# A hybrid trunk layer on one core: the last attention projection goes straight into the merged tiles, stores are queued when due, norm chains enter the order step by step

## The chip, the cores and the metric

One core of one Trainium2 chip. The time is that of one execution of the program in device microseconds (us); of several runs the median is given.

## What is computed

One layer over 2048 rows of width 1024: an input projection to 8208 columns, three branches (forgetting attention with 8 heads of 64, a gated delta rule with 4 heads of 128, attention over 256 memory rows), each gated and projected to width 1024, then merged, projected and normalised.

```
h = rms_norm(x, norm_g);  z = h @ w_in
(aq, ak, av, af, az, bq, bk, bv, ba, bb, bz, mq, mz, gates) = split(z)
o_a = forgetting_attention(aq, ak, av, af + b_fg)      # softmax(q k / 8 + F_q - F_k, causal) v
y_a = o_a * silu(az)
gq, gk, gv = split(silu(causal_dwconv([bq, bk, bv], conv_w)));  gq, gk l2-normalised
y_b = rms_norm(gated_delta_rule(gq, gk, gv, g_log, beta), gdn_norm_g) * silu(bz)
y_m = softmax(mq @ mk / sqrt(128)) @ mv * silu(mz)
proj = einsum('bsnc,ncd->bsnd', stack([y_a, y_b, y_m]), w_branch)
merged = sum(sigmoid(gates + b_merge) * proj, axis=branches)
out = rms_norm(x + merged @ w_out, final_norm_g)
```

## The kernel before

**Numbers.** All is float32. A product is made of three matmuls on rounded parts: high by high, high by low, low by high (`mm3k`, L393). So every operand is split: ScalarE copies the high part, VectorE or GpSimd subtracts it from the source.

**Tiles.** The rows are worked in 4 groups of 512 (g = 0 to 3). Projections are computed transposed, 128 output columns by 512 rows in one PSUM bank, with two banks ("d") in turn for all dense work. What a branch needs later goes by way of DRAM: `dkh`/`dkl` and `dv` for attention, `dgq` for the delta rule, `dgt` for the merge gates, `dya`, `dyb`, `dym` for branch outputs, `dpt` for partly merged sums.

**The order of the work** is set while the program is built. `Plan` (L24) keeps a clock for each engine: TensorE's advances by the work put in, `op`, `act`, `dve`, `pool` (L50 to L62) cost the other engines, and `dma` (L64) costs a transfer by its size at `RATE` = 250 KB per us (L35). Parts are generators; each `yield` names a time before which the part does not go on, and the clock's work. `run` (L79) takes the first part that is due and falls back on the dense stream (`dense`, L324). Each engine, and the queue of SyncE (SP) which issues every DMA, then executes its instructions in that order. `Stores` (L131) holds stores back until their planned time, used before for the projection's outputs alone (`outs`).

**The stages.** `dense` runs the input projection as jobs of 128 columns (weights `wr_in`, `wh_in`, `wl_in`). Beside it run, one after the other (`part_side`, L1282): norm, logits, memory attention, `part_gdn_a` (L720: 16 chunks of 128 rows, transposes `pk`, `pq`, `pv` and products `pa`), `part_gdn_inv` (L818: two inversions of small triangles on VectorE, 31 steps of two instructions each, L831 and L833), `part_gdn_b` (L840: the recurrence over 16 chunks; its `tail`, L970, norms a chunk's output `pO` to `ob` and transposes it to `pR`), and `part_fox` (L1001). This last is the attention: 32 units n = (head h, group G), scores `pst`, output `po` and `pq`, and `sums` (L1131), which adds up a unit's softmax denominators in `pL`, sends them through DRAM (`dL`, `lr`, `rl`, `dR`, `zl`) to turn a row into a column and back, multiplies `oS` by the result and stores it in `dya`.

The dense stream reaches the merge gates (`ev_gate`, L442), whose second half fills the attention's waits, and after them `branch` (L1422) with 8 blocks of 128 columns a group: branch 1 (delta rule) and branch 2 (memory), for each group, add gate times projection to `dpt`. For branch 0 (attention) there are two ways. Groups 0 and 1 go through `branch` too as soon as their attention units are stored: `ev_dram` (L1470) writes the full sum to `dpt[2]`. Groups 2 and 3 wait for the end of the attention and go through `branch_half` (L1538): halves u of 256 rows, two 256-column matmul blocks in one bank `pba`, whose sum is split straight into the merged tiles `mh`, `ml`. `out_half` (L1576) multiplies a half by `w_out` (`pout`), adds x, norms and stores. For groups 0 and 1 `reload_half` (L1569) brings `dpt[2]` back into merged tiles. The order of halves is 4, 5, 6, 7, 0, 1, 2, 3. `load_wo` (L1518) loads `w_out` after the attention ends.

**Loads and stores of a branch block.** `load_gate` (L1447) asks for a gate `gt` and the partial sum `pp` one or two blocks ahead, `gated` (L1459) makes (1 + gate) times the bank on VectorE and adds `pp` on GpSimd, and `ev_dram` puts the store into SP's queue at that place in the order:

```
def ev_dram(n, g, d, ps, ld):
    gt, e, w = gated(ps, ld)
    move(dpt[(n + 1) % 3 // 2 if n else 2][g][:, d, :], gt, 256, w)
    return e
```

`rsqrt` (L282) is a square root on ScalarE and five small VectorE instructions; before, all are put into the order at once, at the place of the call.

Of the kernel before, what the change touches and what calls it, by code (L numbers as in the profile page):

```python
# [18 lines left out]
P = 128  # L19
EPS = 1e-6  # L20
# [3 lines left out]
class Plan:  # L24
# [10 lines left out]
    RATE = 250.0  # L35
# [175 lines left out]
def tile_trunk(ctx, tc, x, mem, norm_g, w_in, w_lg, b_fg, b_mg, conv_w, a_log, dt_b,  # L211
# [69 lines left out]

    def rsqrt(pool, dst, src, n, tag, after):  # L282

        s = pool.tile([P, n], F32, tag=tag + "s", name=tag + "s")
        nc.scalar.activation(s, src, AF.Sqrt)
        r = pool.tile([P, n], F32, tag=tag + "r", name=tag + "r")
        nc.vector.reciprocal(r, s)
        t = pool.tile([P, n], F32, tag=tag + "t", name=tag + "t")
        nc.vector.tensor_mul(t, r, r)
        nc.vector.tensor_mul(t, t, src)  # L290
        nc.vector.tensor_scalar(t, t, -0.5, 1.5, ALU.mult, ALU.add)
        nc.vector.tensor_mul(dst, r, t)
        return pl.op("dve", 0.4, pl.op("act", 1.5, after))
# [23 lines left out]
    def rms_transposed(pool, load, ntile, g_bc, hi, lo, col0, ring, batch, on_dve=(), parts=1):  # L317

        tend = 0.0
        for t0 in range(0, ntile, batch):  # L320
# [22 lines left out]
            t1 = rsqrt(pool, rs, ss, batch, "p0", t1)  # L343
# [376 lines left out]
    def part_gdn_a():  # L720
        with tc.tile_pool(name="ga", bufs=2) as ga:
# [9 lines left out]
            for c in range(NCH):  # L731
# [10 lines left out]
                nc.scalar.activation(gam, gam, AF.Exp)  # L742
                tg = pl.act(512, pl.op("pool", 1.9, td))
# [11 lines left out]
                t1 = pl.op("act", 1.4, pl.pe + pl.LAT)  # L755
# [7 lines left out]
                rg.done(kb, pl.op("act", 1.4, pl.pe + pl.LAT))  # L763
                nc.vector.tensor_scalar(WQ[:, c, :], ssq, EPS, 128.0 * EPS, ALU.add, ALU.mult)
                nc.vector.tensor_scalar(ssk, ssk, EPS, None, ALU.add)
                nc.vector.reciprocal(cs, ssk)
                t1 = rsqrt(ga, rin, ssk, 4, "ga", t1)
                nc.vector.tensor_mul(rin, rin, ssk)
                nc.vector.tensor_mul(cs, cs, Bt[:, c, :])
                nc.vector.tensor_tensor(kds, Gb[:, :, P - 1], Gc, ALU.subtract)  # L770
                nc.scalar.activation(kds, kds, AF.Exp)
                nc.vector.tensor_mul(kds, kds, cs)
                nc.scalar.activation(EGL[:, c, :], Gb[:, :, P - 1], AF.Exp)
                t1 = pl.op("dve", 0.5, pl.op("act", 0.5, t1))
# [65 lines left out]
    def part_gdn_b():  # L840
# [129 lines left out]
        def tail(c, pO, kb, zb):  # L970
# [30 lines left out]
    def part_fox():  # L1001
# [129 lines left out]
        def sums(n, oS, acc, ta):  # L1131
# [16 lines left out]
            st["L"] = n + 1  # L1148
            nc.scalar.copy(oS[96:97], pL[96:97])
# [44 lines left out]
        def values():  # L1194
            for n in range(NU):
# [59 lines left out]
                nc.scalar.copy(oS[0:65], pq[0:65])  # L1255
# [8 lines left out]
                pl.at(tl + 1.0, lambda n=n, oS=oS: move(dL[n][0:1], oS[64:65], 2))  # L1264
# [9 lines left out]
        OB = 4  # L1274
# [49 lines left out]
    def dense():  # L1324
# [95 lines left out]
        YB, GB = 8, 5  # L1420
# [24 lines left out]
        gates = {}  # L1445
# [32 lines left out]
        for d in range(2, 8):  # L1478
            load_wb(1, d)
        seq = [(n, g) for n in (1, 2) for g in range(NG)]  # L1480
        for i, (n, g) in enumerate(seq):
            def mid():
                if i + 1 < len(seq):
                    nxt.append(load_y(*seq[i + 1], range(4)))
            yield from branch(n, g, nxt.pop(0), rd, ev_dram, mid, seq[i + 1] if i + 1 < len(seq) else None)

        def fox_at(n):
            return lambda: 0.0 if state["pv"] >= n else INF

# [12 lines left out]
        for g in range(min(2, NG)):
# [3 lines left out]
            adone[g] = True  # L1506
        yield (lambda: 0.0 if state["fox"] else INF), 0.0
# [10 lines left out]
        def load_wo():  # L1518
            for k in range(KT):
                raw = f3.tile([P, D], F32, tag="ld3", name="wor", bufs=2)  # L1520
                wo[k] = split(woh[:, k], wol[:, k], raw, D, move(raw, w_out[k], 512))
                yield pl.pe + 1.5, 0.0
            move(fg, final_g.partition_broadcast(P), 512)

        pl.add(load_wo())
# [12 lines left out]
        def branch_half(u):  # L1538
            g, v = divmod(u, 2)
            cs = slice(256 * v, 256 * v + 256)  # L1540
            new_merged(u)
            def load_pair(d):
                gt = bp.tile([P, 2, 256], F32, tag="gt", name="gt", bufs=GB)
                move(gt, dgt[g][:, d:d + 2, cs], 256)
                pp = bp.tile([P, 2, 256], F32, tag="pp", name="pp", bufs=3)
                move(pp, dpt[0][g][:, d:d + 2, cs], 256)
# [126 lines left out]
```

## Time and profile before

| | |
|---|---|
| median of 3 runs | 2686.78 us (2686.77 to 2691.32) |
| the profiled execution | 2691.65 us, its span 2689.9 us |
| TensorE busy | 2581.4 us (96%) |
| VectorE, ScalarE, GpSimd busy | 1373.2, 1093.2, 939.2 us |
| moved by DMA | 375.00 MB, mean 139 GB/s |
| mean granted TensorE clock | 0.984 of full speed |

TensorE is busy nearly throughout, so time can come from its idle gaps, from stretches at its lower clock, and from what it computes. A clock of 1.00 in a row is 2.4 GHz, the other level is 1.2 GHz, and a value between is a mean over the stretch. Matmuls overlap: how long one costs is the distance between the starts of two neighbours, not its duration.

### The profile page before, as it was taken

What the parts mean: (1) busy time and instruction counts of PE and PEld (TensorE: products, weight loads), DVE (VectorE), ACT (ScalarE), POOL (GpSimd) and SP (SyncE); (2) the same over time, 40 slices, a digit from 0 to 9 for tenths busy, and PEclk for the clock granted to TensorE, in tenths of its full rate; (3) what the DMA queues carried; (4) which work ended last, traced back from release to release, by engine and by line L of the source; (5) the groups of instructions that cost most, each with busy time, mean ns of one, the idle gap of its engine ahead of it and who ended that gap; (6) DMA issues with size and microseconds to landing.
All of it is one profiled execution on the core that took longest, in us unless ns stands there. A gap on an engine that the chain in (4) does not pass through costs nothing.

```text
span 2689.9 us, 36468 instructions
## 1 busy us (share of the span) xinstructions
PE 2581.4 (96%) x12584; PEld 2124.4 (79%) x12584; DVE 1373.2 (51%) x2813; ACT 1093.2 (41%) x2273; POOL 939.2 (35%) x752
## 2 busy tenths in 40 slices
PE   7999999999999999999999999999999899888998
PEld 5778888888877877878878888888888677767887
DVE  6452566665534484122222086667666776534443
ACT  5442234442565411234333255665566544412221
POOL 0101110011344411122221267777777656753200
PEclk9999999999999999999999999999999999999999
DMA  5223231222566634244543244333332666588443
GB/s 196 72 79 118 73 98 63 75 75 71 196 235 232 213 123 133 93 148 149 166 148 122 98 136 127 113 93 108 114 113 74 207 203 207 171 271 283 147 129 106
DMA packets 264904, 375.00 MB, mean 139 GB/s; under 512 B 62464, under 2 KB 140416, under 8 KB 264464
## 3 DMA queue, kind: packets, MB, share of 16 engines
q1 hardware_dynamic: 264720, 372.68, 43.4%
q8 instruction: 99, 1.62, 0.3%
q14 instruction: 85, 0.70, 0.1%
HBM read 230.66 MB, written 141.92 MB: 139 GB/s over the span
## 4 chain that ended last, share of the span: by engine, by line
PE 74%; DVE 7%; DMA 6%; issue 5%; POOL 4%; ACT 4%; SPq 1%; POOLq 0%; DVEq 0%; ACTq 0%
PE pd_in L395 14%; PE pd_in L397 13%; PE pd_in L396 13%; PE psm L1106 2%; PE pout L1594 2%; PE pout L1593 2%; PE pout L1592 2%; PE pst L1225 2%; PE po L1250 2%; PE pq L1251 2%; PE pst L1224 2%; DVE tmp L831 2%; PE pbr L1436 1%; PE pbr L1437 1%; PE pbr L1438 1%
## 5 line engine op out<-in xcount | busy, mean ns | idle before, releaser
L395 PE MATMUL pd_in<-hh,wh_in 128*128 128x512 f32 x1984 | 803.0, 405 | 18.4 <-DVE evl L425 11.5
L397 PE MATMUL pd_in<-hh,wl_in 128*128 128x512 f32 x1984 | 781.1, 394 | 1.0
L396 PE MATMUL pd_in<-hl,wh_in 128*128 128x512 f32 x1984 | 779.4, 393 | 0.0
L379 POOL TENSOR_TENSOR wl_in<-wr_in,wh_in 128x1024 fp32r<-128x1024 f32 x88 | 213.4, 2425 | 952.0 <-ACT wh_in L375 909.1
L395 PEld LDWEIGHTS pd_in<-hh,wh_in 128*128 128x128 f32 x1984 | 375.8, 189 | 100.3 <-DVE evl L425 14.6
L397 PEld LDWEIGHTS pd_in<-hh,wl_in 128*128 128x128 f32 x1984 | 375.0, 189 | 85.2 <-POOL wl_in L379 4.5
L396 PEld LDWEIGHTS pd_in<-hl,wh_in 128*128 128x128 f32 x1984 | 376.1, 190 | 69.6
L1211 POOL TENSOR_TENSOR acc<-acc,ph 128x512 f32<-128x512 f32 (+3 forms) x288 | 321.8, 1117 | 71.7 <-ACT ph L1231 50.9
L1188 DVE TENSOR_TENSOR plo<-pst,ph 128x512 fp32r<-128x512 f32 (+1 forms) x320 | 192.2, 606 | 100.7 <-ACT pst L1233 98.9
L1231 ACT ACTIVATE ph<-pst 128x512 fp32r<-128x512 f32 (+1 forms) x320 | 170.7, 533 | 154.6 <-PE pst L1225 72.5
L1233 ACT ACTIVATE pst<-pst 128x512 f32<-128x512 f32 (+1 forms) x320 | 170.8, 534 | 0.0
L375 ACT CAST wh_in<-wr_in 128x1024 fp32r<-128x1024 f32 x88 | 92.3, 1049 | 147.5 <-PE pd_in L396 128.5
L1436 PE MATMUL pbr<-yh,wbh 128*128 128x512 f32 x320 | 131.9, 413 | 18.1 <-ACT yh L603 10.3
L1113 DVE TENSOR_REDUCE nmx<-psm 128x1 f32<-128x512 f32 x192 | 128.7, 684 | 24.6 <-PE psm L1106 22.6
L1437 PE MATMUL pbr<-yl,wbh 128*128 128x512 f32 x320 | 128.8, 403 | 0.8 <-DVE yl L604 0.8
L1466 POOL TENSOR_TENSOR gt<-gt,pp 128x512 f32<-128x512 f32 x64 | 85.6, 1340 | 123.7 <-DVE gt L1462 87.8
L1438 PE MATMUL pbr<-yh,wbl 128*128 128x512 f32 x320 | 128.3, 402 | 0.0
L1250 PE MATMUL po<-ph,Vs 128*128 128x512 f32 (+1 forms) x320 | 118.4, 371 | 4.8 <-ACT ph L1231 4.8
L1224 PE MATMUL pst<-QA,KA 128*128 128x512 f32 (+1 forms) x320 | 116.0, 362 | 3.1 <-DVE QA L1121 3.1
L466 DVE SCALAR_TENSOR_TENSOR evv<-xb,cw,evv 128x512 f32<-128x512 f32 x144 | 116.3, 808 | 3.7
L1106 PE MATMUL psm<-KA,QA 68*128 68x512 f32 (+2 forms) x320 | 110.7, 372 | 7.8 <-DVE nmx L1113 7.5
L1251 PE MATMUL pq<-plo,Vs 128*128 128x512 f32 (+1 forms) x320 | 117.6, 370 | 0.2 <-DVE plo L1188 0.2
(331 smaller groups left out, 4372.5 us busy)
## 6 DMA issues: line engine op xcount, KB each, us to landing
wr_in<-in_w_in SPq DMA_DIRECT2D x88, 512.0 KB
dgt<-evg SPq DMA_DIRECT2D x96, 256.0 KB
gt<-dgt SPq DMA_DIRECT2D x96, 256.0 KB
dpt<-gt SPq DMA_DIRECT2D x80, 256.0 KB
pp<-dpt SPq DMA_DIRECT2D x64, 256.0 KB
dgq<-evv SPq DMA_DIRECT2D x48, 256.0 KB
kqv<-dgq SPq DMA_DIRECT2D x16, 768.0 KB
xt<-in_x SPq DMA_DIRECT2D x16, 512.0 KB
```

Of the source, the lines that this page charges most:

```text
L379: nc.gpsimd.tensor_sub(lo, raw, hi.bitcast(F32))
L395: nc.tensor.matmul(ps, wh[:, k, :], xh[:, k, :], start=(k == 0), stop=False)
L396: nc.tensor.matmul(ps, wh[:, k, :], xl[:, k, :], start=False, stop=False)
L397: nc.tensor.matmul(ps, wl[:, k, :], xh[:, k, :], start=False, stop=(k == kt - 1))
L1106: nc.tensor.matmul(ps[:, 0:w], QAn[0:68, j * P:(j + 1) * P], KA[kv(h, ck)][0:68, 0:w], start=True, stop=True)
L1188: nc.vector.tensor_sub(plo[:, 0:w], ps[:, 0:w], ph[:, 0:w].bitcast(F32))
L1211: nc.gpsimd.tensor_add(acc[:, c0:512], acc[:, c0:512], ph[:, 0:w].bitcast(F32))
L1224: nc.tensor.matmul(ps[:, 0:w], KA[kt][:, ks], QAn[:, c0:512], start=True, stop=False)
L1231: nc.scalar.activation(ph[:, 0:w], ps[:, 0:w], AF.Exp, scale=0.125)
L1233: nc.scalar.activation(ps[:, 0:w], ps[:, 0:w], AF.Exp, scale=0.125)
L1250: nc.tensor.matmul(po[:, c0:512], V[:, 0:128], ph[:, 0:w], start=(t0 == 0), stop=(t0 == NT - 1))
L1251: nc.tensor.matmul(pq[:, c0:512], V[:, 64:192], plo[:, 0:w], start=(t0 == 0), stop=(t0 == NT - 1))
```

## The change

The planner's `RATE` goes from 250 to 320. `rsqrt` becomes a generator that yields before its ScalarE and before its VectorE part, each 0.4 us (`AHEAD`) before the time planned; `part_gdn_a` and `tail` yield the same way and cost their squares at 1.9 us, not 1.4. In `part_gdn_a` what does not need the norm goes ahead of it. The last two attention units (`LAST`) compute denominators on the spot, a reciprocal of 64x512 on VectorE, with no trip through DRAM. Branch stores wait in a second `Stores` (`parts`) until due. No group of branch 0 goes through DRAM (`NE = 0`): eight halves in the order 0 to 7, gates and partial sums of the coming blocks loaded ahead across halves, `w_out` loaded two tiles at a time, its low parts on VectorE and GpSimd by turns, the final norm in steps.

```diff
-    RATE = 250.0
+    RATE = 320.0
...
+    AHEAD = 0.4
+
     def rsqrt(pool, dst, src, n, tag, after):
 
+        yield after - AHEAD, 0.0
         s = pool.tile([P, n], F32, tag=tag + "s", name=tag + "s")
         nc.scalar.activation(s, src, AF.Sqrt)
+        after = pl.op("act", 1.6, after)
+        yield after - AHEAD, 0.0
         r = pool.tile([P, n], F32, tag=tag + "r", name=tag + "r")
...
-        return pl.op("dve", 0.4, pl.op("act", 1.5, after))
+        return pl.op("dve", 0.9, after)
...
+            if n >= NU - LAST:
+
+                den = fx.tile([64, 512], F32, tag="zl", name="den", bufs=2)
+                nc.vector.tensor_tensor(den, pL[0:64], oS[64:128], ALU.add)
+                t1 = pl.dve(512, pl.pe + pl.LAT)
+                rs.done(kb, t1)
+                nc.vector.reciprocal(den, den)
+                t1 = pl.op("dve", 4.4)
+                yield t1 - AHEAD, 0.0
+                nc.gpsimd.tensor_mul(oS[0:64], oS[0:64], den)
+                t1 = pl.pool(512, t1)
+                yield t1 - AHEAD, 0.0
+                store(t1)
+                return
...
         def branch(n, g, ys, ring, evac, mid, then=None):
             for d in range(8):
+                yield later(there(W[n, d]), ring.when), 0.0
                 ld = load_gate(n, g, d)
-                yield later(there(W[n, d]), ring.when), 0.0
...
             if (n, g, d) not in gates:
+                parts.leave(GB - 3)
                 gt = bp.tile([P, 512], F32, tag="gt", name="gt", bufs=GB)
...
-            move(dpt[(n + 1) % 3 // 2 if n else 2][g][:, d, :], gt, 256, w)
+            parts.ask(w, lambda: move(dpt[(n + 1) % 3 // 2 if n else 2][g][:, d, :], gt, 256, w))
...
-        for g in range(min(2, NG)):
+        adone[-1] = True
+
+        for g in range(NE):
...
+        parts.leave(0)
+        NH = 2 * NE
+        order = list(range(NH, 2 * NG)) + list(range(NH))
+        pairs, todo = collections.deque(), collections.deque((u, d) for u in range(NH, 2 * NG) for d in range(0, 8, 2))
+        for _ in range(2):
+            load_pair(*todo.popleft())
         yield (lambda: 0.0 if state["fox"] else INF), 0.0
...
-        def load_wo():
-            for k in range(KT):
-                raw = f3.tile([P, D], F32, tag="ld3", name="wor", bufs=2)
-                wo[k] = split(woh[:, k], wol[:, k], raw, D, move(raw, w_out[k], 512))
-                yield pl.pe + 1.5, 0.0
+        wo_feed = Feed(pl, 2)
```

What the order shows at three places; `_123` after a name is the buffer's number.

VectorE in the second triangle inversion. `tmp` and `iv` are the inversion's own, `evl` is the low part of a projected block and frees one of the two dense banks. Before:

```order
L831 TENSOR_TENSOR tmp_8287<-iv_8284,bk_8282 128x23x23
L425 TENSOR_TENSOR evl_8233<-pd_in6_0_3_8200,evh_8231 128x512
L833 TENSOR_REDUCE iv_8284<-tmp_8287 128x23
L831 TENSOR_TENSOR tmp_8287<-iv_8284,bk_8282 128x24x24
L833 TENSOR_REDUCE iv_8284<-tmp_8287 128x24
L831 TENSOR_TENSOR tmp_8287<-iv_8284,bk_8282 128x25x25
L833 TENSOR_REDUCE iv_8284<-tmp_8287 128x25
L425 TENSOR_TENSOR evl_8268<-pd_in7_0_0_8235,evh_8266 128x512
```

Changed, same step of the inversion:

```order
L842 TENSOR_TENSOR tmp_8623<-iv_8620,bk_8618 128x23x23
L844 TENSOR_REDUCE iv_8620<-tmp_8623 128x23
L842 TENSOR_TENSOR tmp_8623<-iv_8620,bk_8618 128x24x24
L844 TENSOR_REDUCE iv_8620<-tmp_8623 128x24
L842 TENSOR_TENSOR tmp_8623<-iv_8620,bk_8618 128x25x25
L844 TENSOR_REDUCE iv_8620<-tmp_8623 128x25
```

Between the first and the last step of the two inversions stood 14 of the 16 `evl` instructions of the k columns, now 2; these jobs have moved ahead, beside `part_gdn_a`, and the dense jobs that now run there (v columns, gates) are read out by ScalarE alone.

ScalarE around the norm of the third chunk in `part_gdn_b` (`jk2` are the four squares of `pO`, `gbs` the root, `evg` a gate block, `wh_in` a weight's high part). Before:

```order
L975 ACTIVATE jk2_9359,so_9358<-pO_9349 128x128 x4
L375 CAST wh_in43_0_9465<-wr_in43_0_9399 128x1024
L285 ACT_TABLE_LOAD
L285 ACTIVATE gbs_9366<-so_9358 128x4
L445 ACT_TABLE_LOAD
```

Changed:

```order
L986 ACTIVATE jk2_9672,so_9671<-pO_9662 128x128 x2
L380 CAST wh_in48_0_9757<-wr_in48_0_9694 128x1024
L986 ACTIVATE jk2_9672,so_9671<-pO_9662 128x128
L450 ACTIVATE evg_9688<-pd_in46_0_1_9600,bmg_73 128x512
L986 ACTIVATE jk2_9672,so_9671<-pO_9662 128x128
L288 ACT_TABLE_LOAD
L288 ACTIVATE gbs_9714<-so_9671 128x4
```

The root stands one readout later on ScalarE; on TensorE 33 dense matmuls of 512 columns stand between `pO` and `pR` of a middle chunk, where 21 stood. ScalarE's table loads in the whole program go from 104 to 113.

SP's queue at the end of the attention (`zl` is the last unit's denominator, `dya3` its store, `yr` a load of attention output, `wbr` of branch weights). Before, last entries ahead of that store:

```order
L243 DMA dpt0_3_134<-gt_21475 128x512
L243 DMA zl_21554<-dR31_263 64x512
L243 DMA wbr_21560<-in_w_br 128x512
L243 DMA wbr_21566<-in_w_br 128x512
L243 DMA yr_21572<-dya0_119 128x512
L243 DMA yr_21578<-dya0_119 128x512
L243 DMA dya3_122<-oT_21188 64x512
```

Changed, the last loads of group 0, 33 entries ahead of that store:

```order
L243 DMA dpt0_2_133<-gt_21082 128x512
L243 DMA yr_21463<-dya0_119 128x512
L243 DMA yr_21483<-dya0_119 128x512
L243 DMA gt_21360<-dgt3_118 128x512
L243 DMA pp_21358<-dpt1_3_138 128x512
L243 DMA dpt0_2_133<-gt_21112 128x512
L243 DMA yr_21579<-dya1_120 128x512
```

`yr` of group 0 no longer stands behind the last denominator. On TensorE 39 matmuls of branch 2 follow the last `pL`, and then `pba` of half 0, where 192 matmuls of `branch(0, 0)` and `branch(0, 1)` stood.

## Rows read from the trace of the kernel before

**Rows 1.** The page, busy time of each engine over the span.

```profile
PE 2581.4 (96%) x12584; PEld 2124.4 (79%) x12584; DVE 1373.2 (51%) x2813; ACT 1093.2 (41%) x2273; POOL 939.2 (35%) x752
```

**Rows 2.** Busy time by stretch: `part_gdn_a`, the inversions, `part_gdn_b`, the attention beside gate jobs, the attention beside branches 1 and 2, the end of branch 2, branch 0 of groups 0 and 1, the start of the halves, the halves, the end. Columns: the stretch, its length, busy us (instructions) of PE, PEld, DVE, ACT, POOL, the granted clock, DMA share, GB/s.

```profile
690.00:930.00 240.00, 232.65 (x1113) 192.13 (x1112) 109.89 (x279) 145.13 (x414) 109.04 (x101) 1.00 0.66 226
930.00:1045.00 115.00, 103.53 (x424) 82.77 (x423) 95.51 (x143) 14.03 (x22) 16.82 (x11) 0.94 0.35 125
...
1110.00:1475.00 365.00, 355.36 (x2155) 298.91 (x2154) 96.82 (x192) 139.55 (x295) 75.71 (x49) 0.99 0.47 143
...
1550.00:2085.00 535.00, 534.87 (x2502) 435.20 (x2501) 372.53 (x865) 318.81 (x634) 390.93 (x338) 1.00 0.37 110
2085.00:2353.00 268.00, 245.91 (x1073) 196.03 (x1071) 182.62 (x362) 122.95 (x253) 167.75 (x145) 0.95 0.65 197
2353.00:2396.40 43.40, 43.34 (x186) 35.45 (x185) 13.88 (x21) 5.52 (x9) 27.21 (x22) 0.97 0.82 268
2396.40:2453.30 56.90, 43.58 (x180) 34.89 (x181) 19.28 (x26) 9.02 (x14) 25.24 (x21) 0.91 0.81 277
2453.30:2484.00 30.70, 25.22 (x169) 23.36 (x168) 15.69 (x19) 10.04 (x13) 8.00 (x6) 0.89 0.84 284
2484.00:2682.10 198.10, 198.03 (x987) 168.55 (x985) 86.88 (x200) 43.70 (x100) 17.14 (x13) 1.00 0.40 134
2682.10:2690.00 7.90, 0.00 (x0) 0.00 (x0) 3.17 (x10) 0.93 (x3) 0.00 (x0) 0.78 0.18 66
```

**Rows 3.** TensorE's waits: who waited for whom, us in total, times, the longest.

```profile
PE pd_in L395 <- DVE evl L425: 11.5, 6, 4.5
PE pbr L1436 <- ACT yh L603: 10.3, 3, 9.0
...
PE pR L988 <- DVE ob L981: 9.4, 10, 2.7
...
PE pbr L1436 <- DVE gt L1462: 7.8, 4, 3.9
PE psm L1106 <- DVE nmx L1113: 7.5, 3, 5.7
```

**Rows 4.** Timeline of TensorE in the second inversion: start, duration, line, matmul, idle time before it.

```profile
1010.06 0.39 PE L396 MATMUL pd_in<-hl,wh_in 128*128 128x512 f32 x1
1010.29 0.39 PE L397 MATMUL pd_in<-hh,wl_in 128*128 128x512 f32 x1
1015.14 0.80 PE L395 MATMUL pd_in<-hh,wh_in 128*128 128x512 f32 x1 [4.47 <-DVE evl L425]
1015.74 0.63 PE L396 MATMUL pd_in<-hl,wh_in 128*128 128x512 f32 x1
1016.16 0.63 PE L397 MATMUL pd_in<-hh,wl_in 128*128 128x512 f32 x1
```

**Rows 5.** Timeline of VectorE at the same place.

```profile
1013.43 1.06 DVE L831 TENSOR_TENSOR tmp<-iv,bk 128x529 f32<-128x529 f32 x1
1014.41 0.68 DVE L425 TENSOR_TENSOR evl<-pd_in,evh 128x512 fp32r<-128x512 f32 x1
```

**Rows 6.** Timelines of ScalarE, VectorE and TensorE in the tail of one chunk of `part_gdn_b`: the first square of `pO`, a weight cast, the table load for the root, a gate readout, `ob`, `pR`.

```profile
1171.87 0.28 ACT L975 ACTIVATE jk<-pO 128x128 f32<-128x128 f32 x1 [3.53 <-PE pO L965]
...
1173.34 1.04 ACT L375 CAST wh_in<-wr_in 128x1024 fp32r<-128x1024 f32 x1
1174.40 1.28 ACT L285 ACT_TABLE_LOAD   x1
1177.21 0.69 ACT L445 ACTIVATE evg<-pd_in,bmg 128x512 f32<-128x512 f32 x1
...
1179.33 0.69 DVE L981 TENSOR_TENSOR ob<-pO,ro 128x512 f32<-128x512 f32 x1
...
1180.16 0.63 PE L988 MATMUL pR<-ident,ob 128*128 128x128 f32 x4 [2.67 <-DVE ob L981]
```

**Rows 7.** Timelines of TensorE and of SP's queue at the end of the attention: the last `pL`, the last denominator's load, a load of group 0, the last store, the first matmul of branch 0.

```profile
2363.97 0.40 PE L1147 MATMUL pL<-al,ones 128*128 128x512 f32 x1
...
2398.16 0.45 SPq L243 DMA_DIRECT2D zl<-dR  x1
...
2400.07 0.80 SPq L243 DMA_DIRECT2D yr<-dya  x2
2403.10 0.47 SPq L243 DMA_DIRECT2D dya<-oT  x1
...
2405.35 0.80 PE L1436 MATMUL pbr<-yh,wbh 128*128 128x512 f32 x1 [9.01 <-ACT yh L603]
```

**Rows 8.** Timeline of TensorE in the first half: two neighbours of 256 columns.

```profile
2453.54 0.28 PE L1564 MATMUL pba<-yh,wbl 128*128 128x256 f32 x1
2453.66 0.28 PE L1562 MATMUL pba<-yh,wbh 128*128 128x256 f32 x1
```

**Rows 9.** Reciprocals on VectorE: times, duration in ns (least, median, most), first and last start, shapes.

```profile
L287 DVE RECIPROCAL gbr<-gbs x16: 177/178/179, 1131.1 to 1467.9; 128x4 f32<-128x4 f32 x16
L287 DVE RECIPROCAL f3r<-f3s x16: 162/164/167, 2499.2 to 2684.2; 128x1 f32<-128x1 f32 x16
```

**Rows 10.** SP's queue: two of the last loads of `w_out`.

```profile
2457.46 1.45 SPq L243 DMA_DIRECT2D wor<-in_w_out  x2
...
2481.67 0.34 SPq L243 DMA_DIRECT2D wor<-in_w_out  x1
```

More of the change, by code (lines that the diff above doesn't have):

```diff
@@ L1479, in dense, with fox_at, load_ya @@
             load_wb(1, d)
+        def fox_at(n):
+            return lambda: 0.0 if state["pv"] >= n else INF
+        ya = {}
+        adone = [False] * (NG + 1)
+        def load_ya():
+            for g in range(NG):
+                yield (lambda: 0.0 if (adone[g - 2] if g > 1 else not g or adone[-1]) else INF), 0.0
+                for k in range(4):
+                    yield fox_at((2 * k + 1) * NG + g + 1), 0.0
+                    ya[g, k] = load_y(0, g, [k])[0]
         seq = [(n, g) for n in (1, 2) for g in range(NG)]
@@ L1506, in dense, with load_pair @@
             adone[g] = True
+        def load_pair(u, d):
+            g, v = divmod(u, 2)
+            cs = slice(256 * v, 256 * v + 256)
+            gt = bp.tile([P, 2, 256], F32, tag="gt", name="gt", bufs=GB)
+            move(gt, dgt[g][:, d:d + 2, cs], 256)
+            pp = bp.tile([P, 2, 256], F32, tag="pp", name="pp", bufs=3)
+            move(pp, dpt[0][g][:, d:d + 2, cs], 256)
+            pairs.append((gt, pp))
+        parts.leave(0)
[4 more added lines that the diff above has]
+            load_pair(*todo.popleft())
         yield (lambda: 0.0 if state["fox"] else INF), 0.0
@@ L1516, in dense, with load_wo, load, use @@
         wo = {}
-        def load_wo():
-            for k in range(KT):
+        wo_feed = Feed(pl, 2)
+        def load_wo(k):
+            def load():
                 raw = f3.tile([P, D], F32, tag="ld3", name="wor", bufs=2)
-                wo[k] = split(woh[:, k], wol[:, k], raw, D, move(raw, w_out[k], 512))
-                yield pl.pe + 1.5, 0.0
-            move(fg, final_g.partition_broadcast(P), 512)
-        pl.add(load_wo())
+                return raw, move(raw, w_out[k], 512)
+            def use(raw):
+                nc.scalar.copy(woh[:, k], raw)
+                t = pl.act(D, pl.pe)
+                lo = nc.gpsimd if k % 2 else nc.vector
+                lo.tensor_sub(wol[:, k], raw, woh[:, k].bitcast(F32))
+                wo[k] = pl.pool(D, t) if k % 2 else pl.dve(D, t)
+            wo_feed.ask(load, use)
+        for k in range(KT):
+            load_wo(k)
+        move(fg, final_g.partition_broadcast(P), 512)
         merged = {}
@@ L1540, in branch_half @@
             cs = slice(256 * v, 256 * v + 256)
+            for k in range(4):
+                yield (lambda: 0.0 if (g, k) in ya else INF), 0.0
             new_merged(u)
[L1542 to L1546, printed above, removed]
-                return gt, pp
-            nxt = load_pair(0)
             for d in range(0, 8, 2):
-                gt, pp = nxt
                 yield ra.when, 0.0
-                if d < 6:
-                    nxt = load_pair(d + 2)
+                if todo:
+                    load_pair(*todo.popleft())
+                gt, pp = pairs.popleft()
                 ps, kb = ra.take("pba")
@@ L1574, in reload_half, with finish @@
                 halves(u, d, 4, t, move(t, dpt[2][g][:, d:d + 4, 256 * v:256 * v + 256], 512))
+        tiles = {"on": 0, "done": 0}
+        def finish(row, xt, s2, e):
+            yield e - AHEAD, 0.0
+            ss = f3.tile([P, 1], F32, tag="ss3", name="ss3", bufs=2)
+            nc.vector.tensor_tensor(ss, s2[:, 0:1], s2[:, 1:2], ALU.add)
+            nc.vector.tensor_scalar(ss, ss, 1.0 / D, EPS, ALU.mult, ALU.add)
+            rs = f3.tile([P, 1], F32, tag="rs3", name="rs3", bufs=2)
+            e = yield from rsqrt(f3, rs, ss, 1, "f3", pl.op("dve", 0.4, e))
+            for hf in range(2):
+                cs = slice(hf * 512, (hf + 1) * 512)
+                nc.vector.scalar_tensor_tensor(xt[:, cs], xt[:, cs], rs, fg[:, cs], ALU.mult, ALU.mult)
+                e = pl.dve(512, e)
+                yield e - AHEAD, 0.0
+                move(out[row:row + P, cs], xt[:, cs], 256, e)
+            tiles["done"] += 1
         def out_half(u):
@@ L1597, in out_half @@
                     ro.done(kb, e)
+                    if jk is None:
+                        jk = f3.tile([P, D], F32, tag="ld3", name="jk3", bufs=2)
                     nc.scalar.activation(jk[:, cs], xt[:, cs], AF.Square, accum_out=s2[:, hf:hf + 1])
                     e = pl.act(512, e)
[L1600 to L1610 removed]
+                pl.add(finish(row, xt, s2, e), True)
         for i, u in enumerate(order):
@@ L1617, in dense @@
                 yield from out_half(order[i - 1])
-            if u == NH - 1:
-                yield from out_half(u)
+        yield from out_half(order[-1])
         bs.close()
```

88 lines of the change are left out of this document (41 added, 47 removed).

## The prediction

> **What bounds the kernel now.** I read the page's busy times first: TensorE works 2581.4 of 2689.9 us, no other engine more than 1373.2 [rows 1]. So I look only for TensorE's idle time, its time at the lower clock, and changes in what it computes. Second, the table by stretch [rows 2], which puts prices on places. Two stretches have nothing to give: the attention beside gate jobs (0.13 us idle in 535) and the halves (0.07 in 198). The others idle for 7.35 (`part_gdn_a`), 11.47 (inversions), 9.64 (`part_gdn_b`), 22.09 (attention beside branches), 13.32 and 5.48 us (branch 0 and start of the halves), and 7.9 after the last matmul. Third, TensorE's waits [rows 3] name who ended them: `evl`, `ob`, `yh`, `gt`, all operations of VectorE and ScalarE that stand in line behind others. Fourth, the timelines of the worst places [rows 4 to 7].
>
> **The clock.** Behind the 4.47 us gap, neighbours of 512 columns start 0.42 us apart, against 0.23 ahead of it [rows 4]: TensorE had idled and then ran at 1.2 GHz for a while. In a stretch of length L with mean granted clock c the loss is (1 - c) x L at most, less what of the low time fell into the gap itself. That is 6.9 us in the inversions, 3.7 in `part_gdn_b`, 13.4 beside the branches, 5.1 and 3.4 in the two stretches at the end [rows 2]. Idle and clock together, at most 102 us lie where this change reaches.
>
> **The change, part by part.**
>
> *Inversions.* The dense stream has two banks. `evl` frees one and stood behind the inversion's instruction of 1.06 us, on which the bank's reader waits its turn [rows 5]; all 11.5 us of `evl` waits [rows 3] agree with the stretch's idle 11.47. The change puts 2 of these `evl` there in place of 14, and the jobs that take their place need ScalarE, which is busy 14.0 of 115 us [rows 2]. Gain 11.5 plus about 5 of the 6.9 of clock; two of fourteen may still wait, 1.5. **-15.** Ends: -16.5 and -8 (if the first long steps meet new readers).
>
> *`part_gdn_a`.* 7.35 us idle at full clock. The steps now stand where they are due, which should shorten waits of readers behind them; but 12 `evl` move in, each able to wait behind one VectorE instruction of 0.69 (as `ob` [rows 6]): 12 x 0.69 = 8.3. **-3**, ends -7.4 and +8.
>
> *`part_gdn_b`.* `pR` waited 9.4 us in ten places for `ob` [rows 3]. From the first square at 1171.87 to the end of `ob` at 1179.33 + 0.69 it took 8.2 us, with a weight cast (1.04) and a table load (1.28) ahead of the root [rows 6]. TensorE's cover between `pO` and `pR` was 21 matmuls of 0.23 [rows 4], 4.8 us, and one small product for four heads (0.6, as `pR`'s [rows 6]); now it is 33, 7.6 us, and three small products, 9.4 in all. In the changed order ScalarE does one readout (0.69) more ahead of the root, so the chain is up to 8.9. It just fits. Gain 9 idle and 2 of the 3.7 clock, 1 left: **-10**, ends -12 and -4. Nine more table loads at 1.28 are 11.5 us of ScalarE, which is busy 139.6 of 365 us here; I put their price below.
>
> *Beside the branches.* Stores no longer stand in SP's queue while their sum is being made, and gates are asked for further ahead: between a gate's buffer and the bank it meets, the buffer numbers, which count what the program creates, differ by 83 on average in branch 2 before and by 103 now. That is against waits such as `gt` (7.8 us in four). But `nmx` (7.5) and part of the `yh` waits [rows 3] come from VectorE and ScalarE holding a split whose load is late, and a planner that believes in 320 KB per us puts that split earlier, not later. Nothing in the trace shows a queue without these stores, so I bound it: between 30 of the stretch's 35.5 won and 15 lost. **-14**, two fifths of the 35.5, since the rows name about that part as `gt` with its clock.
>
> *The end of the attention.* The last unit went from `pL` at 2363.97 to its store at 2403.10, 39 us, of which the queue alone held `zl` until 2398.16; group 0's loads stood behind it and branch 0 began at 2405.35 after 9.01 us of idleness [rows 7]. In the changed order group 0's loads stand 33 entries ahead of the last store and the denominators are made on the spot. Of the two stretches I count 18.8 idle and about 4.7 of the 8.5 us of clock, 23.5. What comes in: 192 matmuls of 512 at 0.23 (44.2 us) become 384 of 256 at 0.12 [rows 8] (46.1): +2. The loads of `w_out`: seven of the eight took 24 us from first to last issue [rows 10] and are needed after eight `pba`, 192 x 0.12 = 23 us, so they are late by some 5 us: +5. **-16**, ends -21 and -8. The reload of the merged halves (8 loads) and the 16 stores to `dpt[2]` vanish, but the halves idle for 0.07 us, so this is worth nothing there.
>
> *The new reciprocals.* 178 ns at 4 columns and 164 at 1 [rows 9] are 4.7 ns a column, so my estimate for 512 is 2.55 us. The first stands in VectorE's line ahead of a bank's readout: add, a small product, reciprocal, readout, 0.7 + 0.7 + 2.55 + 0.7 = 4.7 us against two blocks of branch 2 (5.5 us) before TensorE wants that bank; hidden. The second has 39 matmuls, 9.0 us, to hide behind. So nothing. The Trainium skill ("VectorE: DVE Perf Modes", on the fixed hardware budget) says that a reciprocal repeats its divide step 8 times, which at its 0.96 GHz gives an estimate of 4.3 us for 512 columns and 6.4 for the line; by it the sum would be about 3 us higher, 2640, for a wait of 1 us and its clock. Rows 9 are too small to contradict it.
>
> *What can only get worse.* The attention beside gates has no idle time, and its order changes too; with the nine table loads (11.5 us, half of them ahead of a reader) I put **+8**, ends 0 and +20.
>
> *Start, logits, the last 7.9 us:* their instructions are the same, and the last tile's norm is the same chain: 0.
>
> **The sum:** -15 - 3 - 10 - 14 - 16 + 8 = -50 on the profiled 2691.65, 2641.7. That execution lies 4.9 above the median of 2686.78, which all numbers below go by: 2686.8 - 50 = **2637 us**.
>
> **Rivals.**
> A. *The branches close up almost wholly.* If late stores in the queue were behind most waits, 30 of 35.5 go: 16 more than I count, and with some 4 us from the other terms it is 2637 - 16 - 4 = 2617. For it: 22 us of idleness with DMA at only 0.65 of its time [rows 2]. Against: `nmx` and `yh`.
> B. *The loads are the limit.* A block of branch 2 moves 3 x 256 KB in 12 x 0.23 = 2.76 us, 285 GB/s; the stretches ran at 268 to 284 with 0.81 to 0.84 of DMA time taken [rows 2]. Then nothing is won beside the branches (0 for -14) and `w_out` is 10 us later: 2686.8 - 26 = 2661.
> C. *Slower: branch 2 waits on loads again and again.* The planner's 320 lets splits and readouts be placed as if every load kept up with 285 GB/s, while attention's own loads take their share. A `gt` wait is 1.95 us (7.8 in four) and its low clock 2 to 3 more, 4.5 a wait. It decides from 8 waits among 32 blocks, where 36 us eat what the other terms win; with 16 it is 2686.8 - 36 + 72 = 2723. Against: it had four in 80 blocks, and gates are now loaded further ahead.
> D. *It does not do what it says.* The denominators or the queue are late for another reason and the gaps move on: about 2683.
>
> **How the numbers follow.** The forecast 0.60, A 0.14, B 0.17, C 0.05, D 0.04. The forecast's own range is 2622 to 2652; from A to B gives 2617 to 2661, and the bounds of the branch term and of the order in the attention add some 5 us on either side: 2612 to 2667 leaves out C, D and the far ends. A measurement of this kernel can tell about 0.2%, 5.4 us, from no change. All but C and D are faster by more; three quarters of D lie within it: faster 0.91 + 0.01 = 0.92, same 0.03, slower 0.05.
>
> **What would show it.** Right: no `evl` wait of over 1 us in the inversions and a granted clock of 1.00 there; `pR` waits under 2 us in all; less than 3 us between branch 2's last matmul and `pba`; a gap of at most 5 us at the first `pout`; the attention with branches idle for 10 to 15 us. Wrong: more `gt`, `yh` or `nmx` waits beside the branches than 22 us (B, C); new idleness in the attention beside gates; a `pout` that waits over 10 us for `wol`; or gaps in `part_gdn_a` above 15 us.

## The result, and the profile after

The changed kernel takes 2648.53 us, median of four runs (2646.67 to 2651.28), against 2686.97 for the kernel before: ratio 0.9854, 95% interval 0.9837 to 0.9871. That is 38.4 us less; 50 were forecast, and the time lies within the range. The profiled execution took 2648.26 us. Busy time of each engine, as in [rows 1]:

```profile
PE 2567.6 (97%) x12776; PEld 2122.3 (80%) x12776; DVE 1373.7 (52%) x2817; ACT 1104.8 (42%) x2288; POOL 950.7 (36%) x756
```

The table by stretch, columns as in [rows 2]: `part_gdn_a`, the inversions, `part_gdn_b`, the attention beside gate jobs, beside the branches, the end of branch 2, the first half with the first `pout`, the halves.

```profile
686.00:984.00 298.00, 294.85 (x1395) 244.99 (x1395) 109.65 (x288) 166.55 (x437) 114.93 (x101) 1.00 0.60 204
984.00:1144.00 160.00, 148.91 (x649) 122.56 (x648) 92.38 (x131) 25.48 (x36) 27.46 (x19) 0.97 0.35 121
1144.00:1528.00 384.00, 383.95 (x2308) 323.17 (x2308) 88.47 (x192) 145.82 (x303) 85.40 (x52) 1.00 0.47 145
1541.00:2030.50 489.50, 487.58 (x2279) 395.26 (x2278) 338.41 (x785) 285.65 (x576) 350.59 (x297) 1.00 0.37 109
2030.50:2333.50 303.00, 288.16 (x1274) 229.55 (x1273) 223.88 (x433) 148.70 (x304) 208.77 (x176) 0.97 0.65 198
2333.50:2359.00 25.50, 21.90 (x90) 17.55 (x89) 11.19 (x13) 5.55 (x10) 17.43 (x14) 0.93 0.80 261
2359.00:2397.00 38.00, 30.12 (x207) 28.04 (x206) 17.86 (x22) 12.13 (x19) 21.92 (x17) 0.90 0.85 281
2397.00:2638.90 241.90, 241.84 (x1332) 211.14 (x1330) 101.24 (x226) 50.80 (x115) 40.51 (x27) 0.99 0.39 131
```

Length less PE busy is idleness. `part_gdn_b` has lost all of its 9.6 us and runs at full clock. The inversions have not: 11.1 us idle, as before (11.5). TensorE's waits, to be read beside [rows 3]:

```profile
PE pd_in L400 <- ACT evc L417: 9.5, 1, 9.5
...
PE ptm L1133 <- DVE mt L1129: 4.5, 2, 2.4
PE pout L1667 <- ACT woh L1574: 4.1, 1, 4.1
PE psm L1119 <- DVE nmx L1126: 4.0, 6, 1.2
...
PE pbr L1466 <- DVE gt L1493: 3.6, 1, 3.6
PE pba L1616 <- DVE gt L1493: 3.1, 2, 2.2
...
PE pd_in L400 <- DVE evl L430: 1.8, 2, 1.6
```

`ob` is gone and `evl` is down from 11.5 to 1.8, but one wait of 9.5 for `evc`, the readout of a v block, is new. It is in the second inversion; timelines of TensorE, ScalarE and SP's queue there:

```profile
1092.84 0.39 PE L402 MATMUL pd_in<-hh,wl_in 128*128 128x512 f32 x1
1102.76 0.80 PE L400 MATMUL pd_in<-hh,wh_in 128*128 128x512 f32 x1 [9.54 <-ACT evc L417]
```

```profile
1082.43 0.59 ACT L417 COPY evc<-pd_in 128x512 f32<-128x512 f32 x1 [4.85 <-PE pd_in L402]
1102.12 0.59 ACT L417 COPY evc<-pd_in 128x512 f32<-128x512 f32 x1 [19.11 <-DMA dv<-evc]
```

```profile
1061.28 5.76 SPq L243 DMA_DIRECT2D dv<-evc  x2
1096.73 0.32 SPq L243 DMA_DIRECT2D dinv<-iv  x1
1097.14 0.38 SPq L243 DMA_DIRECT2D dv<-evc  x1
```

From 1067 to 1096.73 us the queue issues nothing: at its head stands the store of the inversion's result, which VectorE finishes at 1096.7. The v stores behind it hold all three `ev` tiles, so ScalarE has nowhere to read the next bank to, and TensorE no bank.

The end, TensorE as in [rows 7]: last `pL`, last matmul of branch 2, first of the halves, and the first `pout` that waits.

```profile
2349.90 0.40 PE L1160 MATMUL pL<-al,ones 128*128 128x512 f32 x1
...
2358.76 0.39 PE L1468 MATMUL pbr<-yh,wbl 128*128 128x512 f32 x1
2358.99 0.28 PE L1616 MATMUL pba<-yh,wbh 128*128 128x256 f32 x1
...
2392.74 0.79 PE L1667 MATMUL pout<-woh,mh 128*128 128x512 f32 x1 [4.06 <-ACT woh L1574]
```

### The profile page after: what moved, and what is told of

Read it like the earlier page. It is cut to its first block, busy times and chain, and to the rows that moved or that the text cites. A ratio compares the mean times of both kernels' runs of the same rounds, so it can differ in the third digit from the quotient of the medians.

```text
span 2646.5 us, 36843 instructions
## 1 busy us (share of the span) xinstructions
PE 2567.6 (97%) x12776; PEld 2122.3 (80%) x12776; DVE 1373.7 (52%) x2817; ACT 1104.8 (42%) x2288; POOL 950.7 (36%) x756
## 4 chain that ended last, share of the span: by engine, by line
PE 79%; DVE 6%; DMA 5%; POOL 4%; issue 3%; ACT 2%; SPq 1%; POOLq 0%; DVEq 0%; ACTq 0%
PE pd_in L400 15%; PE pd_in L402 15%; PE pd_in L401 15%; PE pout L1668 2%; PE pout L1669 2%; PE pout L1667 2%; DVE tmp L842 2%; PE pst L1253 2%; PE psm L1119 2%; PE pst L1252 2%; PE po L1278 2%; PE pq L1279 2%; DVE iv L844 1%; POOL acc L1239 1%; POOL wl_in L384 1%
## 5 line engine op out<-in xcount | busy, mean ns | idle before, releaser
L1253 PE MATMUL pst<-QB,KB 128*128 128x512 f32 (+1 forms) x320 | 117.0, 367 | 0.0
L1466 PE MATMUL pbr<-yh,wbh 128*128 128x512 f32 x256 | 105.5, 412 | 5.6 <-DVE gt L1493 3.6
L1667 PE MATMUL pout<-woh,mh 128*128 128x512 f32 x256 | 100.4, 395 | 4.1 <-ACT woh L1574 4.1
```

The costliest lines, as they stand in the source:

```text
L1253: nc.tensor.matmul(ps[:, 0:w], KB[kt][:, ks], QBn[:, c0:512], start=False, stop=True)
```

## The experiments

Each was timed beside the kernel before on the same chip (ratios with their 95% intervals), except e4, a single execution. The table gives, from the records of each profiled execution, TensorE's loss in us: its idle time, and what matmuls at the lower clock took beyond the usual distance of their neighbours. Stretches end at the first `pk`, the last `pa`, the first `pB`, the last `pR`, the first `pbr` and the last `pout`. The columns don't add up to the times: what a matmul takes longer without a wait and outside the recorded low clock stands in no row. Between two profiled executions this comes to as much as 9 us (e8 loses 22.9 less than before and is 13.8 shorter; e12 loses 20.5 more than e7 and is 12.9 longer), so a difference of a few us between two columns says little.

| | before | after | e2 | e3 | e6 | e7 | e8 | e12 |
|---|---|---|---|---|---|---|---|---|
| start | 39.8 | 33.2 | 35.8 | 35.1 | 37.1 | 32.1 | 38.2 | 34.2 |
| `part_gdn_a` | 7.4 | 3.2 | 3.1 | 0.7 | 3.2 | 0.7 | 1.1 | 1.3 |
| inversions | 17.3 | 12.7 | 1.6 | 22.3 | 1.6 | 0.0 | 19.1 | 0.8 |
| `part_gdn_b` | 12.8 | 0.1 | 0.1 | 0.0 | 0.0 | 0.0 | 17.5 | 0.0 |
| attention beside gates | 1.8 | 2.5 | 2.9 | 3.1 | 2.4 | 4.5 | 5.6 | 5.9 |
| branches and halves | 54.8 | 38.8 | 38.3 | 36.1 | 54.4 | 39.2 | 29.5 | 54.8 |
| median, us | 2687.0 | 2648.5 | 2636.9 | 2654.7 | 2653.1 | 2635.2 | 2676.6 | 2650.1 |

**e1, the changed kernel again.** 

> The changed kernel once more, as the base of the runs beside it. 2648.5 us (2646.7 to 2651.3 in four runs so far). If the 9.54 us gap at the end of the second inversion comes from the order of SP's queue, which is fixed in the program, it is there again within 1 us; if it was an accident of one execution, it is under 3 us.

2648.26 us, ratio 0.9857 (0.9839 to 0.9875). The gap is there again, 9.52 us: it is in the program's order.

**e2, the inversions' stores late.**

```diff
-        nc.sync.dma_start(dst, src)
+        pl.last = nc.sync.dma_start(dst, src).ins
...
-                t1 = move(dinv[s], iv.rearrange("p t j i -> p t (j i)"), 1024, pl.dve(1024, t1))
+                with tc.issue_after(pl.last): t1 = move(dinv[s], iv.rearrange("p t j i -> p t (j i)"), 1024, pl.dve(1024, t1))
```

> The changed kernel, with the two stores of the inversions' results put into SP's queue behind every transfer that the program has issued before them (TensorE, VectorE and ScalarE keep their order). Theory: the store of the second inversion stood at the head of the queue from 1067 to 1096.73 us, no v store could pass, the three readout buffers stayed full, ScalarE sat idle for 19.1 us and TensorE for 9.54. Then that gap goes, with 1.6 us at the lower clock behind it: 2648.5 - 11 = 2637.4, the inversions idle for under 2 us. Rival: TensorE waits there for VectorE's inversion anyway, or the later U and dd loads make the recurrence start late: no gain, 2647 to 2650, and a new gap of some 10 us at the first pB.

2636.88 us, 0.9811 (0.9795 to 0.9827): 11.4 under e1, as the theory says. The inversions by stretch, and SP's queue at the store:

```profile
985.00:1134.70 149.70, 148.15 (x654) 122.34 (x653) 92.68 (x132) 25.42 (x36) 27.68 (x19) 1.00 0.37 131
```

```profile
1102.21 5.20 SPq L243 DMA_DIRECT2D dgt<-evg  x2
...
1111.81 0.32 SPq L243 DMA_DIRECT2D dgt<-evg  x1
1112.22 0.38 SPq L243 DMA_DIRECT2D dinv<-iv  x1
```

Idle for 1.55 us at full clock, where it was 11.1 at 0.97. The store now leaves behind the readouts' stores, and no wait comes in its place.

**e3, the chains in steps alone.** The kernel before, with the hunks of the diff for `rsqrt`, `part_gdn_a` and `tail`.

> The kernel before, with only the step by step chains: rsqrt as a generator, the new order and costs in part_gdn_a and in tail. Nothing else of the change. In the order the evl between the inversions' steps go from 14 to 0, and the second inversion's store stands behind 14 of the 16 v stores, not behind 11 as in the whole change. Theory (the three stretches of the delta rule gain by these steps alone): part_gdn_a -4, the inversions -5 to -15, part_gdn_b -13 against 2687.0, nothing elsewhere: 2687 - 24 = 2663, range 2655 to 2667; pR waits under 2 us in all. Rival: what removed these waits was the transfer rate in the planner, which moved the dense jobs: 2680 or more, with pR waiting for ob 9 us.

2654.7 us, 0.988 (0.9861 to 0.9899): 32 us won, more than the theory's 24, although the inversions got worse. The rival is out: with `RATE` at 250 the waits of `pR` are gone (`part_gdn_b` loses 0.0). TensorE, SP's queue and GpSimd there:

```profile
1102.62 0.39 PE L401 MATMUL pd_in<-hl,wh_in 128*128 128x512 f32 x1
1122.44 0.79 PE L402 MATMUL pd_in<-hh,wl_in 128*128 128x512 f32 x1 [19.44 <-POOL wl_in L384]
```

```profile
1076.05 5.76 SPq L243 DMA_DIRECT2D dv<-evc  x2
1111.86 0.32 SPq L243 DMA_DIRECT2D dinv<-iv  x1
```

```profile
1116.17 0.95 POOL L855 MEMSET dd<- 128x1024 f32 x1 [42.81 <-DMA dinv<-iv]
...
1120.05 4.66 POOL L384 TENSOR_TENSOR wl_in<-wr_in,wh_in 128x1024 fp32r<-128x1024 f32 x2
```

The same store again, but through another engine: GpSimd's first work for the recurrence waits for it, and the weight split that TensorE needs stands behind that. What the theory left out is the last row of the table: the branches and the end lose 36 us, not 55, though no load, store or half there was touched.

**e4, denominators through DRAM** (`LAST = 0`). 

> The changed kernel, with the last two units' denominators sent through DRAM as those of all other units are; all halves stay. Theory: the trip took 39 us from the last pL to the store in the kernel before; branch 2 covers 9 us of it, so the first half, whose tiles lie in memory that the attention frees, starts some 30 us late: 2648.5 + 30 = 2678, one gap of 20 to 30 us at the first pba or pout. Rival: the first half needs only groups 0 and 1, stored long before, so the trip hides behind halves 0 to 5: 2646 to 2652, no gap above 5 us there.

2657.11 us in a single execution, 8.9 over e1, whose four executions lie 6.4 apart. Neither size: if the last trip costs something, it is far less than the 39 us of [rows 7], and no gap at `pba` or `pout` reaches 4 us (`pba` for `wbh` 3.9; `pout` for `wol` 4.9 in four). No wait names the trip, so it hides; that loads and weight splits, which the planner puts off until the attention has ended, come later by it is not shown.

**e5, e6: the rate, and the branch stores,** both on e2. e5 sets `RATE = 250`; e6 puts the stores into the queue at once:

```diff
-            parts.ask(w, lambda: move(dpt[(n + 1) % 3 // 2 if n else 2][g][:, d, :], gt, 256, w))
+            move(dpt[(n + 1) % 3 // 2 if n else 2][g][:, d, :], gt, 256, w)
```

> The changed kernel with the inversions' stores put late (as in e2_inv_store_late, 2636.9 us) and the planner's RATE back at 250. In e3_before_with_gdn_steps, which has 250, the attention beside the branches lost 15 us to idleness and low clock, with 320 it loses 26 to 29. Theory: a planner that believes in 320 KB per us puts splits and readouts ahead of what the loads can feed, and that is the difference: about -12, 2625 us, the stretch idle for 12 to 15 us. Rival: the difference comes from the halves or from the queue of branch stores, and the rate does nothing: 2634 to 2640, the stretch idle for over 17 us.

2642.04 us, 0.9824 (0.981 to 0.9839): 5 over e2, with intervals that overlap. The theory is wrong: beside the branches TensorE idles for 18.1 us, the lower rate gains nothing, and `woh` waits at `pout` grow from 2.9 to 12.7. The rival has the idleness right and the time 2 us too low.

> The changed kernel with the inversions' stores put late (2636.9 us), its branch stores put into SP's queue where the sum is made, as before the change. Theory of the prediction (stores in the queue while their sum is made hold the next gate's load): the waits for gt and yh beside the branches grow by about what was counted as won, +8 to +14: 2645 to 2651. Rival (e3_before_with_gdn_steps queues them at once and idles less there): no loss, 2631 to 2640.

2653.1 us, 0.9867 (0.9852 to 0.9882): 16 over e2. In this order the queue of stores is worth what the prediction had in mind and a little more, but not by the waits that the theory named: those of `pbr` for a gate fell from 6.9 us in e2 (the first line below, and 1.7 for the load itself) to 0.9. The loss came out in the waits for `nmx` and `QA`, and for weight splits (the other lines, e6):

```profile
PE pbr L1466 <- DVE gt L1493: 5.2, 2, 5.0
...
PE psm L1119 <- DVE nmx L1126: 8.1, 6, 5.7
PE pout L1668 <- POOL wol L1577: 4.3, 2, 2.4
PE pba L1618 <- POOL wbl L1427: 4.2, 2, 2.3
PE pst L1252 <- DVE QA L1134: 3.7, 1, 3.7
```

The longest, 5.7, is ScalarE on a split whose load was late (`yh`, idle 6.33 for `yr<-dym`), with the attention's work behind it.

**e7, e8: what each half of the change does alone.** e7 is e3 with the edit of e2. e8 is the whole change with `rsqrt`, `part_gdn_a` and `tail` as before.

> The kernel before with the step by step chains alone (e3, 2654.7 us) and the inversions' stores put late. In e3 the second store stood at the head of SP's queue from 1082 to 1111.9 us, GpSimd waited for it and TensorE for a weight split behind GpSimd's wait, 19.4 us. Theory: that gap and 2.9 us of low clock go: 2654.7 - 22 = 2632.5, under the whole change with the same mending (2636.9), so that the rest of the change is worth nothing or costs 4. Rival: the wait is GpSimd's or VectorE's own and moves to the first product of the recurrence: 2645 to 2655.

2635.18 us, 0.9801 (0.9785 to 0.9818), the fastest of all, with e2 (0.9795 to 0.9827) beside it. The chains in steps and a store in the right place give 52 us; queue, rate and halves on top of them (e2) give nothing that can be told.

> The whole change without the step by step chains of part_gdn_a, tail and the norms (rsqrt as before); rate 320, queued branch stores, eight halves, denominators on the spot. Theory (the terms add): what is left of the change is 2648.5 - 2654.7 = -6 against 2687: 2677 to 2684, with evl waits of 10 us in the inversions and pR waits of 9 us. Rival: by the prediction's terms the branches and the end of the attention win 30 less 8 of their own: 2657 to 2667.

2676.59 us, 0.9954 (0.9939 to 0.9969): beside e3 the terms add, within some 5 us (32.3 and 10.4 for e3 and e8, 38.4 for the change). With the store late they don't: e7 wins 51.8 and e2, with this half on top, 50.1. The waits are back as said (`evl` 13.4, `ob` 13.0), while branches and halves lose only 29.5: alone, that half of the change wins up to 25 there, but gives 5 back to `part_gdn_b` and 4 to the attention, and its time falls by 10 in all.

**e9 to e11: other mixtures.** e9 is e7 with the queue of branch stores; e11 is e9 with `RATE = 320`; e10 is e2 with `NE = 2`.

> e7_gdn_steps_store_late (the kernel before, chains in steps, inversions' stores late: 2635.2 us) and the queue of branch stores of the change, nothing else of it. Theory: what the queue was worth in the whole change (e6 less e2, 2653.1 - 2636.9 = 16) it is worth here too, since the stores stand in the same way in SP's queue: 2619 to 2623, and the gt waits of branch 2 and branch 0 (5.8 and 4.0 us) under 2. Rival: the queue pays only in the order that the change gives, where branch 2 ends straight at the halves; here the 12 us of idleness come from nmx and QA and stay: 2632 to 2638.

> The changed kernel with the inversions' stores late (2636.9 us), and groups 0 and 1 of branch 0 by way of DRAM again (NE = 2, halves in the order 4 to 7, 0 to 3), with queued stores, rate 320 and denominators on the spot. Theory of the prediction (no group by DRAM lets the attention's end go under branch 2): of the 16 counted there the denominators keep about 9 (e4 less e1), so some 5 to 8 are lost: 2641 to 2645. Rival: 192 matmuls of branch 0 cover the loads of w_out and of the gates, at which the first half waits 7 us in e2, and nothing comes in their place: 2627 to 2634.

> e9 with the planner's RATE at 320. Theory: the rate is worth about 5 (e5 less e2, 2642.0 - 2636.9): 2614 to 2630, 5 under e9. Rival: those 5 were the late w_out at the first pout (8.1 and 4.6 us in e5), which this order doesn't have: within 3 us of e9.

e9 2637.26 (0.9818, 0.9803 to 0.9833), e10 2643.58 (0.9835, 0.9816 to 0.9853), e11 2642.51 (0.984, 0.9823 to 0.9858). The queue that was worth 16 in e6 is worth nothing in e9, as its rival said. The rate gains nothing in e11, which lies 5 over e9, outside theory and rival, with intervals that overlap. e10 is 6.7 over e2, as the prediction's theory had it, but again the intervals overlap. With e2, e5 and e7 these three lie within 8.4 us; of the versions with the late store so far only e6 stands apart.

**e12, the branches moved back.** e7 with one cost of the planner, at its two places:

```diff
-                t1 = pl.op("act", 1.9, pl.pe + pl.LAT)
+                t1 = pl.op("act", 1.4, pl.pe + pl.LAT)
...
-                t2 = pl.op("act", 1.9, pl.pe + pl.LAT)
+                t2 = pl.op("act", 1.4, pl.pe + pl.LAT)
```

> e7_gdn_steps_store_late (2635.2 us) with the planner's cost of the squares in part_gdn_a back at 1.4 us from 1.9; the steps and the late stores stay. In the order the dense matmuls beside part_gdn_a go from 1140 to 1113, and of the branch matmuls 321 then stand after the last pL, as in the kernel before, not 210 as in e7. Theory: the steps won beside the branches and at the end, 55 to 39 us, because more of the branch work lies under the attention, whose matmuls give its loads time; with 321 outside again that comes back: 2635 + 13 = 2648, range 2644 to 2652, the delta rule within 4 us of e7. Rival: it is the steps' finer order on the engines, or chance from arrangement to arrangement, and not where the branch work lies: 2632 to 2640.

2650.1 us, 0.9861 (0.9842 to 0.9879). The delta rule stays as in e7, and branches and halves lose 54.8, to the tenth what they lost before. The old gap is back; TensorE and SP's queue in e12:

```profile
2352.93 0.39 PE L1451 MATMUL pbr<-yh,wbl 128*128 128x512 f32 x1
2363.03 0.79 PE L1449 MATMUL pbr<-yh,wbh 128*128 128x512 f32 x1 [9.72 <-ACT yh L608]
```

```profile
2356.27 0.45 SPq L243 DMA_DIRECT2D zl<-dR  x1
...
2357.89 0.91 SPq L243 DMA_DIRECT2D yr<-dya  x2
```

As in [rows 7], group 0's last loads stand behind the last denominator (`zl`). In e7 they left 57 us ahead of it:

```profile
2309.86 0.91 SPq L243 DMA_DIRECT2D yr<-dya  x2
...
2367.53 0.45 SPq L243 DMA_DIRECT2D zl<-dR  x1
```

The time is the one that the theory gave (2648). But of the 15.6 us between e12 and e7 only 4 lie behind the last `pL`, where the theory looked for them, since in e7 two `gt` waits of 5.8 and 4.0 stand in place of the gap; 11.6 lie beside the attention (30.4 against 18.8), in small waits and their low clock. So the runs show that the order of the dense work, which one cost in `part_gdn_a` changed here, is enough to bring the loss back. They don't show that it does so by how many matmuls lie behind the attention, and the rival, chance from arrangement to arrangement, is not ruled out. That stays open.

## Why the prediction was right, and where it was not

The time lies within the range, 12 us over the forecast, and its make-up is right only in part. Inversions and branches gave 26 us less than forecast; the +8, which hardly came, and the start, put at nothing, gave 14 of it back, and `part_gdn_a` and `part_gdn_b` 4 more. That the errors cancelled so far is luck. From trace to trace (43.4 us; the profiled execution of before is 4.7 above its median):

| term | forecast | measured |
|---|---|---|
| start | 0 | -6.6 |
| `part_gdn_a` | -3 | -4.2 |
| inversions | -15 | -4.6 |
| `part_gdn_b` | -10 | -12.7 |
| branches, end of attention, halves | -14 - 16 | -16.0, +1.8 for the narrower matmuls |
| what can only get worse | +8 | +0.7 beside gates |

The measured rows add up to 41.6; the other 1.8 us stand in none.

*Start.* The prediction put it at nothing, but the first norm's `rsqrt` yields now too. Versions with the chains in steps lose 32 to 37 there, e8, without them, 38.2. e1 and after, one kernel, are some 2 apart. How much of the 6.6 is the norm's order and how much the spread of executions isn't shown.

*Inversions: the step that failed.* "The jobs that take their place need ScalarE, which is busy 14.0 of 115 us": it asked whether the reader had time and not who frees the tile it writes to. The `evl` went as said; their gain was given back to a store at the head of SP's queue (e1, and e2, which gets the 11 us back). The queue's order has that store behind eleven of the sixteen v stores; in e2, where it is held behind the transfers that the code asks for ahead of it, it stands behind all sixteen. The rows of the changed order would have shown it before any run.

*`part_gdn_b`.* Right: the cover of 33 matmuls is enough, `pR` waits for nothing, and e3 and e8 show that it is the steps. 2.7 more came since no chain was late.

*Branches: the term furthest off.* "Beside the branches" and "end of attention" gave half of their 30. Split at the last `pL`, with two rows each for before, after and e7 (columns as in [rows 2]):

```profile
2093.00:2364.00 271.00, 250.90 (x1089) 201.00 (x1090) 180.52 (x356) 117.84 (x242) 167.07 (x144) 0.95 0.65 197
2364.00:2682.10 318.10, 299.17 (x1475) 253.25 (x1473) 131.60 (x260) 67.69 (x135) 70.63 (x53) 0.97 0.57 189
...
2040.80:2349.90 309.10, 293.21 (x1292) 234.63 (x1292) 222.86 (x431) 144.32 (x295) 213.54 (x180) 0.97 0.66 202
2349.90:2638.90 289.00, 281.06 (x1577) 246.70 (x1575) 124.96 (x253) 64.65 (x135) 67.34 (x47) 0.98 0.47 155
...
2028.70:2335.60 306.90, 294.91 (x1310) 235.99 (x1311) 219.27 (x433) 145.57 (x296) 215.14 (x180) 0.98 0.69 208
2335.60:2626.40 290.80, 274.27 (x1364) 231.83 (x1362) 122.70 (x246) 62.01 (x126) 55.57 (x41) 0.98 0.54 179
```

Beside the attention TensorE idled for 20.1 us before and 15.9 after, so the -14 brought 4.2 of idleness and, by the granted clock, at most 4 more. Behind the last `pL` it idled for 18.9 and now 7.9: that term came mostly as forecast. What failed in the first is the wait that it was sized by. [rows 3] count the whole program; of the 7.8 us of `gt` only two waits lie beside the branches, and after the change one of 3.6 us is left (its line stands in the section on the result). Those two, from 2020 to 2420 us in the kernel before:

```profile
PE pbr L1436 <- DVE gt L1462: 4.2, 2, 3.9
```

So stores out of the queue and gates asked for further ahead took 0.6 us from the waits that they were meant for. e6 shows that the queue can matter (16), though not by these waits, and e9 that it need not.

e3 and e7, without queue, rate or halves, lose as little in all as the whole change (36 and 39 against 39), but win it elsewhere: e7 idles for only 12.0 beside the attention and still 16.5 behind it. And e12, with one planner cost of the delta rule changed back, loses the old 54.8. What the prediction did not ask is what the delta rule's new order does 900 us later: it takes in dense jobs sooner (1140 dense matmuls beside `part_gdn_a` in e7, 756 before), the branches start earlier against the attention, 210 branch matmuls are left after the last `pL` in e7, not 321, and group 0's loads come ahead of the last denominators. How much each of these gives is open (e12).

*The end.* As said: no wait at the first `pba`, 4.1 us at the first `pout`, for `w_out` as forecast. e4 would put the denominators on the spot at about 9 of the 16, by its single execution.

*The reciprocals.* Nothing, as said, though each took longer than my 2.55 us:

```profile
L1174 DVE RECIPROCAL den<-den x2: 3341/3342/3344, 2301.8 to 2351.7; 64x512 f32<-64x512 f32 x2
```

The waits behind them stay covered: TensorE has no gap of over 0.2 us from 2299.2 to 2336 us, behind the first, nor from 2340.4 to 2373, behind the second. The Trainium skill ("VectorE: DVE Perf Modes", on the fixed hardware budget) led to an estimate of 4.3 us; the measured 3.34 lies between that and mine, and decides.

*The rivals.* A did not come. B came near beside the branches, which won little, but not by its reason: e8, with the same loads, loses only 29.5 in branches and halves, and `w_out` was late by 4 us and not by 10 more. C did not come, 3.6 us of `gt` in branch 2. D came in kind in one stretch, the inversions, where the gap moved to another wait. Of what the prediction set as signs, `pR`, `pba` and `pout` came out right. The idleness beside the branches did so only by where the stretch is cut: 14.8 us in the table's, 18.4 when it is taken on to the last `pL`. The inversions failed both of theirs: an `evl` of 1.55 us, a clock of 0.97.

## What to carry to other kernels

When a wait is taken from an engine, ask not only whether the next reader has time but which store frees the tile that it writes, and what stands ahead of that store in the queue. A change early in a kernel moves what lies under what much later: here it took 16 to 19 us of loss from a stretch that it did not touch (e7, e3), and edits meant for that stretch then won nothing more. A sum that comes out right proves none of its terms; each needs its own run.

## What the runs showed of the hardware

A reciprocal of 64x512 took 3342 ns, against 164 for one column [rows 9]: 6.2 ns a column, where the small shapes gave 4.7.

Single VectorE instructions of the inversions ran some 1.3 to 2 us over their neighbours, at other steps in each inversion; from the second inversion after the change:

```profile
1050.51 0.16 DVE L842 TENSOR_TENSOR tmp<-iv,bk 128x4 f32<-128x4 f32 x1
...
1050.90 2.21 DVE L842 TENSOR_TENSOR tmp<-iv,bk 128x9 f32<-128x9 f32 x1
...
1053.34 0.19 DVE L842 TENSOR_TENSOR tmp<-iv,bk 128x16 f32<-128x16 f32 x1
```

What causes it was not tried.
